# A first TensorE job in four chunks, and a new list schedule, in a hybrid decoder block

## The chip, the cores and the metric

The kernel runs on one core of a Trainium2 chip. The metric is the device time of one execution in microseconds (us). TensorE (PE in the profile, PEld its weight loads) multiplies matrices, VectorE (DVE) and ScalarE (ACT) work element by element, SyncE (SP) and GpSimd (POOL) mostly issue transfers (DMA) between memory and the on-chip buffers. TensorE writes its results into eight banks, which VectorE and ScalarE read.

## The reference

One decoder layer over 512 tokens of width 1024, with 256 memory tokens; every input is fp32.

```python
h = _rmsnorm(x, norm_mix_g)
p_a, p_b, q, p_g = jnp.split(h @ w_in, IN_SPLITS, axis=-1)
gb, gc, v = jnp.split(p_a, 3, axis=-1)
y_a = (gb * _causal_dwconv(gc * v, conv_a_w)) @ w_a_out
u, ug = jnp.split(p_b, 2, axis=-1)
u = _causal_dwconv(u * jax.nn.sigmoid(ug), conv_b_w) + conv_b_bias      # 31 taps
y_b = jax.nn.silu(_layernorm(u, ln_b_g, ln_b_b)) @ w_b_out
k, vm = jnp.split(_rmsnorm(mem, norm_mem_g) @ w_kv, 2, axis=-1)
y_c = attention(q, k, vm) @ w_att_out                                   # 4 heads
g = jax.nn.sigmoid(p_g + b_gate)
x = x + (g[0] * y_a + g[1] * y_b + g[2] * y_c) @ w_o
gt, up = jnp.split(_causal_dwconv(_rmsnorm(x, norm_ffn_g) @ w_up, conv_ffn_w), 2, axis=-1)
x = x + (jax.nn.silu(gt) * up) @ w_down
return _rmsnorm(x, norm_final_g)
```

The block touched first is `_rmsnorm(mem, norm_mem_g) @ w_kv`: the keys and values of the memory tokens.

## The kernel before, in words

**Split operands.** Each fp32 operand is split into a high part (a cast to fp32r) and a low part (the operand minus the high part). ScalarE makes the high part (whi of weights, mh of the memory block), VectorE the low part (wlo, ml). A product is then three matmuls: high by high, high by low, low by high. For weights a "unit" is a tile of 128x1024 loaded into one of six load buffers (wf); whi and wlo have four buffers each. The helper split_job makes the two jobs ("wh", unit) and ("wl", unit), at lines 495 and 499.

**Seven products for eight.** The large projections (w_in and w_up in quads of four blocks, w_o, w_down) use seven block products, numbered 1 to 7, in place of eight, on sums and differences of operands and weights. The sums of weights are mostly made by transfers that add (jobs s5, s6, s7, s3 on POOL, line 633). The jobs r1 to r7 (lines 702 to 723) read the banks into results. A job of TensorE in a quad is 24 matmuls (line 675).

**The planner.** All work is put into a table of jobs with engine, cost, what it follows and which buffers it takes. TensorE's jobs have a fixed order, and from it each other job gets a due time, the latest start that keeps TensorE going. Then a list scheduler places jobs one at a time: the one that can start earliest, and among equals the one with the earliest due time. This gives each engine's program order, which the chip then follows with waits on semaphores. Two tables change the result, both by kind of job, a key such as "SP ld up u". LATER adds so many us to a due time and so moves the job back (or, if negative, forward) in the ranking. A kind in AHEAD may not start earlier than so many us before its due time. A kind that is in neither starts as soon as it can. "NONE" jobs take no engine; "temps" closes the buffers of the mixer and opens those of the up projection.

**The start.** jobs.first is a hand-written list of the first loads; their due times are their place in it less its length, to which LATER is added. TensorE begins with a warm-up of nine matmuls (18 records, line 1766), then the first key job K(0,0), the first value job V(0,0), V(0,1), K(1,0), K(0,1) and so on. K(0,0) multiplies the first half of the transposed memory (mem block 0, four pieces of 128x256: index i or k) by the first unit of w_kv. Both arrive as two loads of 256 KB each. For the memory block the jobs ("mh", g, e) and ("ml", g, e) treat two pieces at a time (lines 765 and 772). halved_unit (line 859) does the same for K(0,0) and V(0,0): loads, casts (line 873) and low parts (line 877) in halves of 128x512. pe_keys (line 964) cuts K(0,0) into two TensorE jobs of 12 matmuls, each behind its own half.

```python
job(("mh", g, e), "ACT", 2 * scaled_act(256), mem_high,
    [("ldm", g, e)] + ([("mh", g, 0)] if e else []), use=[("mem", g)])
...
for e in range(2):
    pe(K0 if e else ("K0",), 12 * MM_QUAD,
       lambda e=e: keys_product(0, 0, (2 * e, 2 * e + 1)), [("wl0", "K", e), ("ml", 0, e)],
       take=[] if e else [(bank, "ps")], use=[bank] if e else [], unit=e == 1)
```

keys_product (line 929 holds its matmul) runs over the two halves of the result and, in each, over the pieces it was given.

## Time and profile before

| | |
|---|---|
| median of 3 runs | 925.8 us (925.8 to 926.52) |
| profiled execution, its own time | 925.64 us |
| its span, first to last instruction | 923.8 us |
| mean granted TensorE clock | 0.999 |
| instructions | 16764 |
| first product of K(0,0), last matmul | 5.30 us, 917.86 us |

Times in the profile count from the span's start. "L929" is line 929 of the kernel. A row of the timeline has start, length, engine, line, operation, what is written from what, the shapes, and how many instructions were merged; in brackets stands how long the engine idled before and what ended it. Tile names are the program's: mem and mh/ml belong to the memory block, wf to a loaded weight unit, whi/wlo to its parts, fb00 to ft7 to the seven forms of the activations (an h or l behind for the part), bank to an accumulator. SPq rows are transfers being issued.

### The profile page before, as it was taken

The page shows a single profiled execution, that of the slowest core. Times are in us where ns is not written, and L with a number is a line of the kernel's source. Part 1 is how long each engine was busy: PE and PEld are TensorE (multiplying, and loading weights), DVE is VectorE, ACT ScalarE, POOL GpSimd, SP SyncE. Part 2 cuts the span into 40 slices and gives each one's busy share as a digit, 9 for nine tenths or more (in the row PEclk, how much of TensorE's full clock was granted, in tenths as well). Part 3 has the DMA queues.
Part 4 walks back from the last instruction along what each step waited for, and adds up shares of the span by engine and source line. Part 5 has one row for each costly group of instructions (what it writes and reads, how often), then busy time and mean ns, then how long its engine had stood idle before and what let it go on. Part 6 is the DMA issues. An engine that isn't in the chain of part 4 may idle for free.

```text
span 923.8 us, 16764 instructions
## 1 busy us (share of the span) xinstructions
PE 916.6 (99%) x6677; PEld 862.8 (93%) x6677; DVE 837.4 (91%) x953; ACT 671.0 (73%) x911; POOL 126.5 (14%) x153
## 2 busy tenths in 40 slices
PE   9999999999999999999999999999999999999997
PEld 8999999999989999999899888899999999988886
DVE  6897999989989999999986779898999889999987
ACT  7567988879977887788746743777766676765656
POOL 0121121101111211110100001021221121003300
PEclk9999999999999999999999999999999999999999
DMA  9999689666787879788956598499999877789962
GB/s 364 367 252 199 151 178 205 167 160 137 194 188 205 183 168 213 174 210 201 220 108 173 157 322 187 114 227 307 279 248 226 207 142 149 197 266 338 244 131 92
DMA packets 54366, 190.60 MB, mean 206 GB/s; under 512 B 6160, under 2 KB 6544, under 8 KB 54288
## 3 DMA queue, kind: packets, MB, share of 16 engines
q0 software_dynamic: 20880, 75.24, 45.2%
q1 hardware_dynamic: 33120, 114.02, 34.7%
q8 instruction: 52, 0.85, 0.3%
q10 hardware_dynamic: 288, 0.27, 0.1%
q14 instruction: 26, 0.21, 0.1%
HBM read 185.31 MB, written 4.19 MB: 205 GB/s over the span
## 4 chain that ended last, share of the span: by engine, by line
PE 95%; DMA 2%; DVE 1%; issue 0%; ACT 0%; POOL 0%; DVEq 0%; POOLq 0%; ACTq 0%
PE bank L675 57%; PE bank L448 7%; PE bank L446 7%; PE bank L447 7%; PE bank L1418 5%; PE bank L1417 5%; PE bank L1419 5%; PE bank L929 2%; DMA wf<-in_w_up 2%; PE bank L1766 0%; PE ss L802 0%; DVE wlo L499 0%; PE bank L1166 0%; DVE upc L1373 0%; DVE gtc L1373 0%
## 5 line engine op out<-in xcount | busy, mean ns | idle before, releaser
L495 ACT CAST whi<-wf 128x1024 fp32r<-128x1024 f32 (+1 forms) x199 | 206.9, 1044 | 97.7 <-PE bank L675 39.3
L499 DVE TENSOR_TENSOR wlo<-wf,whi 128x1024 fp32r<-128x1024 f32 (+1 forms) x193 | 232.4, 1211 | 29.8 <-ACT whi L495 29.6
L1238 ACT ACTIVATE tp<-u,pk 128x510 f32<-128x510 f32 (+22 forms) x184 | 119.4, 704 | 7.0 <-DVE acc L1245 6.9
L1245 DVE TENSOR_TENSOR acc<-acc,tp 128x1020 f32<-128x1020 f32 (+22 forms) x92 | 109.2, 1188 | 6.0 <-ACT tp L1238 5.0
L633 POOL DMA_DIRECT2D wf<-in_w_in x51 | 45.1, 890 | 245.1 <-DVE wlo L499 160.2
L675 PE MATMUL bank<-ft6h,wlo 128*128 128x256 f32 x232 | 64.3, 277 | 0.1
L675 PE MATMUL bank<-fb10h,whi 128*128 128x256 f32 x232 | 64.4, 278 | 0.0
L675 PE MATMUL bank<-fb00h,whi 128*128 128x256 f32 x232 | 64.4, 278 | 0.0
L675 PE MATMUL bank<-ft6h,whi 128*128 128x256 f32 x232 | 64.4, 277 | 0.0
L675 PE MATMUL bank<-ft7h,whi 128*128 128x256 f32 x232 | 64.3, 277 | 0.0
L675 PE MATMUL bank<-ft7l,whi 128*128 128x256 f32 x232 | 64.3, 277 | 0.0
L675 PE MATMUL bank<-ft7h,wlo 128*128 128x256 f32 x232 | 64.3, 277 | 0.0
L675 PE MATMUL bank<-fb00l,whi 128*128 128x256 f32 x232 | 64.3, 277 | 0.0
L675 PE MATMUL bank<-fb11h,whi 128*128 128x256 f32 x232 | 64.3, 277 | 0.0
L675 PE MATMUL bank<-fb00h,wlo 128*128 128x256 f32 x232 | 64.3, 277 | 0.0
L675 PE MATMUL bank<-ft5h,wlo 128*128 128x256 f32 x232 | 64.3, 277 | 0.0
L675 PE MATMUL bank<-ft5h,whi 128*128 128x256 f32 x232 | 64.3, 277 | 0.0
L675 PE MATMUL bank<-ft5l,whi 128*128 128x256 f32 x232 | 64.3, 277 | 0.0
L675 PE MATMUL bank<-ft6l,whi 128*128 128x256 f32 x232 | 64.2, 277 | 0.0
L675 PE MATMUL bank<-fb10h,wlo 128*128 128x256 f32 x232 | 64.2, 277 | 0.0
L675 PE MATMUL bank<-fb10l,whi 128*128 128x256 f32 x232 | 64.2, 277 | 0.0
L675 PE MATMUL bank<-fb11l,whi 128*128 128x256 f32 x232 | 64.1, 276 | 0.0
(388 smaller groups left out, 3146.1 us busy)
## 6 DMA issues: line engine op xcount, KB each, us to landing
wf<-in_w_in SPq DMA_DIRECT2D x55, 512.0 KB, 5.1
wf<-in_w_in POOLq DMA_DIRECT2D x51, 512.0 KB, 6.2
wf<-in_w_up SPq DMA_DIRECT2D x29, 512.0 KB, 5.7
wf<-in_w_up POOLq DMA_DIRECT2D x28, 512.0 KB, 6.1
wf<-in_w_down SPq DMA_DIRECT2D x15, 512.0 KB, 3.7
wf<-in_w_att_out SPq DMA_DIRECT2D x8, 512.0 KB, 4.5
wf<-in_w_a_out SPq DMA_DIRECT2D x8, 512.0 KB, 4.2
wf<-in_w_b_out SPq DMA_DIRECT2D x8, 512.0 KB, 4.3
```

The costliest lines, as they stand in the source:

```text
L446: nc.tensor.matmul(ps, s_hi, w_hi, start=start, stop=False, skip_group_check=again)
L447: nc.tensor.matmul(ps, s_hi, w_lo, start=False, stop=False, skip_group_check=again)
L448: nc.tensor.matmul(ps, s_lo, w_hi, start=False, stop=stop, skip_group_check=again)
L495: nc.scalar.copy(parts[0], src())
L499: nc.vector.tensor_tensor(lo, src(), hi.bitcast(F32), op=ALU.subtract)
L633: nc.gpsimd.dma_start(out=tiles[key], in_=block(w, col[c], k), accum_op=ALU.add)
L675: nc.tensor.matmul(ps[:, c, :], w[:, k, at], a[k], start=first and n == 0, stop=i == 3 and n == 2, skip_group_check=again,)
L1238: nc.scalar.activation(two(("tp", p, s))[:, j, s:], two(("u", p))[:, j, : SEQ - s], AF.Copy, scale=weight(j),)
L1245: nc.vector.tensor_tensor(a, a, two(("tp", p, s))[:, :, s:], op=ALU.add)
L1417: nc.tensor.matmul(ps, w_hi[:, i, at], hi, start=first, stop=False)
L1418: nc.tensor.matmul(ps, w_hi[:, i, at], lo, start=False, stop=False)
L1419: nc.tensor.matmul(ps, w_lo[:, i, at], hi, start=False, stop=last)
```

## The change

Four edits of the code, and new tables:

1. For both memory blocks the jobs mh and ml are defined for each of the four pieces, not for two at a time. The instructions are the same, eight a side; other work can be placed between them.
2. halved_unit takes a number of pieces: the casts and low parts of K(0,0) are in quarters of 128x256 (four and four instructions for two and two), those of V(0,0) stay halves. The loads stay halves.
3. K(0,0) is four TensorE jobs of six matmuls, one for each piece k, each behind its own ("wl0", "K", k) and ("ml", 0, k). The 24 matmuls are the same; their order is now by piece, then by half of the result.
4. Later jobs on the memory blocks wait for the last piece, ("ml", g, 3), or for the second piece of their pair.
5. The tables LATER and AHEAD are replaced. LATER had 33 entries and has 39, AHEAD had 8 and has 15.

```diff
--- before.py
+++ after.py
@@ -70,19 +70,21 @@
 
 
 LATER = {
-    "ACT r1 cv": -198, "ACT r1 gate": -73, "ACT r5 gate": -106, "ACT tap 1": -3.62,
-    "ACT tp 3": -101, "ACT vh": 37, "ACT wh merge 2": -5, "ACT wh mix 5": 117,
-    "DVE fl h2 t4": 1.22, "DVE fl h2 t7": -5, "DVE h t5": 56, "DVE h2 t4": -19, "DVE kl": -60,
-    "DVE low": -20, "DVE r2 up": 19, "DVE tap 2": -32, "DVE tap 3": 136, "DVE wl up 6": -90,
-    "DVE wl up 7": -30, "DVE x1 c": -46, "DVE xnorm": 97, "SP ld K 0": -4, "SP ld V 0": -6,
-    "SP ld mix r": 13, "SP ld mix u": 12, "SP ld mix v": 10.92, "SP ld up r": -18,
-    "SP ld up s": -23.22, "SP ld up u": -64, "SP ld up v": -34, "SP ld0 K": -102,
-    "SP ld0 V": -5.56, "SP ldm": -4,
+    "ACT fh h2 t7": 5, "ACT r4 glu": -10, "ACT r5 glu": 284, "ACT sigmoid": 19.8,
+    "ACT tp 3": -37.08, "ACT wh mix 2": 109, "ACT wh up 5": 96, "DVE CV": -29, "DVE h t7": 109,
+    "DVE kl": 27, "DVE kt": 65, "DVE ql": -145, "DVE r3 cv": -1, "DVE r3 glu": 38,
+    "DVE r3 q": -26, "DVE r7 gate": -15, "DVE tap 2": -44, "DVE vl": 189, "DVE wl V 0": -4,
+    "DVE wl mix 1": -22, "DVE wl mix 2": -11, "DVE wl mix 5": 30, "DVE wl up 6": -24,
+    "DVE xnorm": 85, "NONE temps": 25, "POOL s5 glu": 30, "POOL s5 up": 6.66, "SP ld K 0": 3,
+    "SP ld e 0": -7, "SP ld mix r": 11, "SP ld mix s": -6, "SP ld mix v": 6, "SP ld up r": -42,
+    "SP ld up s": -43, "SP ld up u": -64, "SP ld up v": -44, "SP ld wo 0": -41, "SP x1b": 58,
+    "SP xl": 8,
 }
 
 AHEAD = {
-    "ACT r1 glu": 5, "ACT tap 1": 150, "ACT vh": 5, "DVE kl": 10, "DVE low": 10, "DVE tot1": 40,
-    "POOL wadd e": 5, "POOL xa": 10,
+    "ACT fh h2 t7": 10, "ACT mgh g": 5, "ACT r5 cv": 40, "ACT sigmoid": 40, "ACT tp 3": 40,
+    "DVE CV": 80, "DVE r3 cv": 5, "DVE r3 glu": 40, "NONE temps": 20, "POOL s3 q": 5,
+    "POOL s5 glu": 40, "POOL s5 up": 20, "SP ld e 0": 10, "SP x1b": 80, "SP xl": 20,
 }
 
 
@@ -756,29 +758,29 @@
                 out=tiles["mem", g][:, 512 * e : 512 * (e + 1)], in_=mem_t[2 * g + e]),
                 [("mem tile", g)], LOAD_LATENCY, use=[("mem", g)])
 
-            def mem_high(g=g, e=e):
-                if e == 0:
-                    for part, side in (("mh", "h"), ("ml", "l")):
-                        tiles[part, g] = forms.tile(
-                            [P, 4, HALF], F32R, tag=MEM_PLACE[g] + side, name=name(part))
-                for i in range(2 * e, 2 * e + 2):
+
+            for i in range(2 * e, 2 * e + 2):
+                def mem_high(g=g, i=i):
+                    if i == 0:
+                        for part, side in (("mh", "h"), ("ml", "l")):
+                            tiles[part, g] = forms.tile(
+                                [P, 4, HALF], F32R, tag=MEM_PLACE[g] + side, name=name(part))
                     nc.scalar.activation(
                         tiles["mh", g][:, i, :], four(("mem", g))[:, i, :], AF.Copy,
                         scale=par("norm_mem_g", 4 * g + i),
                     )
 
-            def mem_low(g=g, e=e):
-                for i in range(2 * e, 2 * e + 2):
+                def mem_low(g=g, i=i):
                     nc.vector.scalar_tensor_tensor(
                         tiles["ml", g][:, i, :], four(("mem", g))[:, i, :],
                         par("norm_mem_g", 4 * g + i), tiles["mh", g][:, i, :].bitcast(F32),
                         op0=ALU.mult, op1=ALU.subtract,
                     )
 
-            job(("mh", g, e), "ACT", 2 * scaled_act(256), mem_high,
-                [("ldm", g, e)] + ([("mh", g, 0)] if e else []), use=[("mem", g)])
-            job(("ml", g, e), "DVE", 2 * 0.4, mem_low,
-                [("mh", g, e)] + ([("ml", g, 0)] if e else []), use=[("mem", g)])
+                job(("mh", g, i), "ACT", scaled_act(256), mem_high,
+                    [("ldm", g, e)] + ([("mh", g, i - 1)] if i else []), use=[("mem", g)])
+                job(("ml", g, i), "DVE", 0.4, mem_low,
+                    [("mh", g, i)] + ([("ml", g, i - 1)] if i else []), use=[("mem", g)])
 
         def mem_square(g=g):
             make(("msq", g))
@@ -856,7 +858,7 @@
 
     K0, V0 = ("K", 0, 0), ("V", 0, 0)
 
-    def halved_unit(unit, src, n_k):
+    def halved_unit(unit, src, n_k, pieces):
         s, raw, parts = unit[0], ("raw", unit), []
         job(("raw tile", s), "NONE", 0.0, lambda: make(raw), take=[(raw, "wf")])
         for e in range(2):
@@ -865,25 +867,27 @@
                 out=tiles[raw][:, at], in_=src[:, at]), [("raw tile", s)],
                 LOAD_LATENCY, use=[raw])
 
-            def high(e=e, at=at):
-                if e == 0:
+        width = 1024 // pieces
+        for i in range(pieces):
+            def high(i=i, at=slice(width * i, width * (i + 1))):
+                if i == 0:
                     parts.extend(
                         wts.tile([P, 1024], F32R, tag=s, name=name(s)) for s in ("whi", "wlo"))
                     w_units[unit] = [t.rearrange("p (k n) -> p k n", k=n_k) for t in parts]
                 nc.scalar.copy(parts[0][:, at], tiles[raw][:, at])
 
-            def low(at=at):
+            def low(at=slice(width * i, width * (i + 1))):
                 hi, lo = parts
                 nc.vector.tensor_tensor(
                     lo[:, at], tiles[raw][:, at], hi[:, at].bitcast(F32), op=ALU.subtract
                 )
 
-            job(("wh0", s, e), "ACT", actv(512), high,
-                [("ld0", s, e)] + ([("wh0", s, 0)] if e else []), use=[raw])
-            job(("wl0", s, e), "DVE", dve(512), low, [("wh0", s, e)], use=[raw])
-
-    halved_unit(K0, block(w_kv, 0, 0), 4)
-    halved_unit(V0, w_v[0, 0], 2)
+            job(("wh0", s, i), "ACT", actv(width), high,
+                [("ld0", s, 2 * i // pieces)] + ([("wh0", s, i - 1)] if i else []), use=[raw])
+            job(("wl0", s, i), "DVE", dve(width), low, [("wh0", s, i)], use=[raw])
+
+    halved_unit(K0, block(w_kv, 0, 0), 4, 4)
+    halved_unit(V0, w_v[0, 0], 2, 2)
 
     for hp in range(2):
         for kp in range(4):
@@ -946,7 +950,7 @@
 
     def pe_values(hp, kp):
         banks = [("bank", "V", hp, c) for c in range(MC)]
-        take, lows = [(b, "ps") for b in banks], [("ml", kp // 2, kp % 2)]
+        take, lows = [(b, "ps") for b in banks], [("ml", kp // 2, 2 * (kp % 2) + 1)]
         if (hp, kp) == (0, 0):
             for e in range(2):
                 pe(V0 if e else ("V0",), 6 * MM, lambda e=e: values_product(0, 0, e),
@@ -964,13 +968,13 @@
     def pe_keys(h, g):
         bank = ("bank", "K", h)
         if (h, g) == (0, 0):
-            for e in range(2):
-                pe(K0 if e else ("K0",), 12 * MM_QUAD,
-                   lambda e=e: keys_product(0, 0, (2 * e, 2 * e + 1)), [("wl0", "K", e), ("ml", 0, e)],
-                   take=[] if e else [(bank, "ps")], use=[bank] if e else [], unit=e == 1)
+            for k in range(4):
+                pe(K0 if k == 3 else ("K0", k), 6 * MM_QUAD,
+                   lambda k=k: keys_product(0, 0, (k,)), [("wl0", "K", k), ("ml", 0, k)],
+                   take=[] if k else [(bank, "ps")], use=[bank] if k else [], unit=k == 3)
         else:
             pe(("K", h, g), 24 * MM_QUAD, lambda: keys_product(h, g, range(4)),
-               [("wl", ("K", h, g)), ("ml", g, 1)], take=[] if g else [(bank, "ps")],
+               [("wl", ("K", h, g)), ("ml", g, 3)], take=[] if g else [(bank, "ps")],
                use=[bank] if g else [])
```

## The prediction

> **What bounds the kernel now.** I read the busy line of the page first, then the waits of TensorE, then the busy time by stretch.
>
> ```profile
> PE 916.6 (99%) x6677; PEld 862.8 (93%) x6677; DVE 837.4 (91%) x953; ACT 671.0 (73%) x911; POOL 126.5 (14%) x153
> ...
> PE bank L1766 <- POOL ident masks.py:199: 1.4, 1, 1.4
> ...
> 0.00:5.30 5.30, 3.94 (x19) 3.92 (x19) 0.91 (x3) 3.00 (x5) 0.77 (x8) 1.00 0.67 201
> 5.30:9.13 3.83, 3.83 (x26) 3.60 (x25) 3.48 (x6) 2.88 (x6) 0.00 (x0) 1.00 1.03 398
> ...
> 598.00:643.00 45.00, 45.00 (x383) 44.67 (x381) 39.57 (x45) 33.51 (x47) 8.61 (x10) 1.00 0.99 265
> ...
> 918.00:923.80 5.80, 0.13 (x2) 0.00 (x0) 2.13 (x5) 1.52 (x4) 0.00 (x0) 0.84 0.72 271
> ```
>
> In the stretches the columns are length, then busy time and count for PE, PEld, DVE, ACT and POOL, then clock, DMA share and GB/s. TensorE is the bound almost without a hole. Its only listed wait is before the warm-up, and from 598 to 643 us, where the transfers are densest, it is busy the whole time. A busy PE can still hide a pause of a few tenths, because the ends of matmuls are modelled, so from here on I compare starts. The number of matmuls is the same after the change, so there are three places to win: the start (first product at 5.30), pauses between neighbouring starts, and the end after the last matmul (918 to 923.8), which the edit of the code doesn't touch.
>
> The start, with all engines in order of time (start, length, engine; SPq rows are loads being issued):
>
> ```profile
> 0.74 0.39 SPq L755 DMA_DIRECT2D mem<-in_mem_t  x1
> 1.19 0.89 SPq L864 DMA_DIRECT2D wf<-in_w_kv  x2
> 1.36 4.21 PE L1766 MATMUL bank<-ident 128*128 128x128 f32 x18 [1.36 <-POOL ident masks.py:199]
> 2.12 0.43 SPq L755 DMA_DIRECT2D mem<-in_mem_t  x1
> 3.83 0.91 ACT L765 ACTIVATE mh<-mem,pk 128x256 fp32r<-128x256 f32 x2 [1.50 <-DMA pk<-in_packed]
> 4.64 0.60 ACT L873 CAST whi<-wf 128x512 fp32r<-128x512 f32 x1
> 5.28 0.69 DVE L877 TENSOR_TENSOR wlo<-wf,whi 128x512 fp32r<-128x512 f32 x1
> 5.30 0.58 PE L929 MATMUL bank<-mh,whi 128*128 128x256 f32 x1
> 5.59 0.62 ACT L873 CAST whi<-wf 128x512 fp32r<-128x512 f32 x1 [0.34 <-DMA wf<-in_w_kv]
> 5.68 0.41 PE L929 MATMUL bank<-ml,whi 128*128 128x256 f32 x1
> 6.02 0.58 PE L929 MATMUL bank<-mh,wlo 128*128 128x256 f32 x1
> 6.40 0.41 PE L929 MATMUL bank<-mh,whi 128*128 128x256 f32 x1
> 6.62 0.41 PE L929 MATMUL bank<-ml,whi 128*128 128x256 f32 x1
> 7.04 0.33 PE L929 MATMUL bank<-mh,whi 128*128 128x256 f32 x1
> 7.21 0.28 PE L929 MATMUL bank<-ml,whi 128*128 128x256 f32 x1
> 7.32 0.28 PE L929 MATMUL bank<-mh,wlo 128*128 128x256 f32 x1
> 9.13 0.39 PE L446 MATMUL bank<-whi,mh 128*128 128x512 f32 x1
> ```
>
> The first product starts just after the first half of whi is done (4.64 + 0.60 = 5.24). The third needs wlo, done at 5.28 + 0.69 = 5.97, and starts at 6.02. Starts are 0.22 apart until about 7.04 and 0.11 apart from 7.21 on. The 24 products of the first job end where V0 begins, at 9.13.
>
> **The chunks.** With four pieces the first job waits for a quarter of each operand. Two rows price a 128x256 piece:
>
> ```profile
> 621.05 0.41 ACT L596 CAST ft4x<-h2b 128x256 fp32r<-128x256 f32 x1
> 625.08 0.42 DVE L601 TENSOR_TENSOR ft4x<-h2b,ft4x 128x256 fp32r<-128x256 f32 x1
> ```
>
> So a quarter of the weight unit costs 0.41 us on ScalarE and 0.42 on VectorE, where a half costs 0.60 to 0.62 and 0.69. Over the unit that is 4 x 0.41 - 2 x 0.61 = 0.42 us more ScalarE and 4 x 0.42 - 2 x 0.69 = 0.30 us more VectorE. The memory block keeps its eight instructions a side; only their order is free now. The first chain becomes: mh piece from 3.83, whi piece about 4.25 to 4.65 (its load had landed by 4.64), wlo piece about 4.8 to 5.2. All of it is done before 5.30. The warm-up's 18 records, some 0.22 us apart from 1.36, occupy TensorE until about 5.2 to 5.3, so the first product stays at 5.2 to 5.3; I take 5.30. The second stays at 5.68, since a weight load is exposed there (5.30 to 5.68 is 0.38, against 0.22 in the row after). The third no longer waits for wlo: 5.68 + 0.22 = 5.90 for 6.02, and the fourth, which before paid the same exposed load after the wait (6.02 to 6.40), comes at 6.12, 0.28 us earlier.
>
> What becomes of the 0.28 depends on the slow stretch. If it ends at 7.04 whatever TensorE has done, products 4 to 8 still come 0.22 apart, the eighth at 7.00 where it was at 7.21, and from there the lead is about 0.2. If it ends after a number of products, the lead stays 0.28, and 0.38 with a first product at 5.2. The lower end is nothing, if a later quarter waits; I take 0.25, between the first two.
>
> By the Trainium skill, "TensorE: Matmul & The Clock Gate", section "What's actually happening", the slow clock lasts for a budget of time and not for a number of matmuls, so removed idle time in it buys only half of itself. By that rule the sum would have the 0.2, by the count the 0.28. The trace shows one end of the slow spacing, at about 7.1, and can't tell the two apart.
>
> The later quarters mustn't wait. The list of first loads ranks the second part of the memory block ahead of the second half of K0 now that the shift of -102 on "SP ld0 K" is gone (in the rows above both K0 halves left at 1.19 and the block's second part at 2.12). The half that arrived at 5.59 then arrives one 256 KB slot later, 0.26 MB / 398 GB/s = 0.66 us: about 6.25. Then whi pieces 3 and 4 end by about 7.2 and the last wlo piece by 7.7 on VectorE; quarter 3 of TensorE starts near 7.6 and wants its wlo near 7.85, quarter 4's is wanted near 8.5. No wait, with about 0.4 us to spare; the bound of a loss here is the 0.66 slot itself.
>
> **The loads behind it.** The shifts on "SP ldm" and "SP ld K 0" change too: -4 for both before; none and +3 now. So the second memory block (two loads) goes ahead of the weights K(1,0).
>
> ```profile
> 4.02 0.43 SPq L525 DMA_DIRECT2D wf<-in_w_kv  x1
> 4.50 1.11 SPq L755 DMA_DIRECT2D mem<-in_mem_t  x2
> ...
> 10.88 1.03 ACT L495 CAST whi<-wf 128x1024 fp32r<-128x1024 f32 x1
> 11.82 0.90 ACT L765 ACTIVATE mh<-mem,pk 128x256 fp32r<-128x256 f32 x2
> 11.95 1.23 DVE L499 TENSOR_TENSOR wlo<-wf,whi 128x1024 fp32r<-128x1024 f32 x1 [0.67 <-ACT whi L495]
> ...
> 14.86 0.28 PE L929 MATMUL bank<-mh,wlo 128*128 128x256 f32 x1
> ```
>
> K(1,0) was cast at 10.88, so it had landed; behind 0.52 MB more it lands at most 0.52 / 398 = 1.3 us later, 12.2. Its wlo was done at 13.18 and would be by 14.5; it is wanted at 14.86 - 0.25 = 14.61. That is cover of 0.1 us, and mh pieces of 0.41 that slip in front eat it. The cost lies between 0 and some 1.0 us (two such pieces on each engine); I take 0, since the transfers lost to K(1,0) bring the memory block's own work forward into the idle time of ScalarE.
>
> **The new list schedule.** It touches the priorities of some sixty kinds of jobs, moves no matmul and issues no instruction more; what it can cost is a wait of TensorE. The place with least to spare is the start of the up projection, where the transfers have a DMA share of 0.99 (first fence):
>
> ```profile
> 609.67 0.59 ACT L702 COPY gt<-bank 128x512 f32<-128x512 f32 x1
> ...
> 610.57 8.41 DMA wf<-in_w_up
> ...
> 642.12 1.23 DVE wlo L499
> ...
> 601.62 0.28 PE L675 MATMUL bank<-fb10h,whi 128*128 128x256 f32 x1
> 620.34 0.28 PE L675 MATMUL bank<-ft6h,whi 128*128 128x256 f32 x1
> 642.99 0.28 PE L675 MATMUL bank<-ft6l,whi 128*128 128x256 f32 x1
> 643.39 0.38 PE L675 MATMUL bank<-ft6h,wlo 128*128 128x256 f32 x1
> ```
>
> At 643.39 TensorE starts 0.40 after its neighbour instead of 0.11: 0.29 us lost to a wlo that ended at 643.35. So the split of (up 2, product 6) has no cover at all, and the edit changes its shift ("DVE wl up 6" from -90 to -24), those of the four kinds of up loads, and holds back "temps", after which the first banks of the up projection are read. That hold can be worked out from the code: the read at 609.67 must let the bank of (up 0, product 2), which starts at 601.62 and lasts 2.8, be read within 8 us of its end; that makes its due time about 601.6 + 2.8 + 8 - 1.4 = 611 (1.4 is what the code's costs give the read and the add behind it), and +25 - 20 moves it to 616. The bank is written again at 620.34, so about 4 us are left: no cost by itself. What is queued behind it on ScalarE and VectorE moves later with it, towards 642. For the whole schedule the bounds are a gain of 0.29 (that pause gone) and a loss of one landing, 8.4 us. I take 0 for the forecast.
>
> **The sum.** Profiled execution: 925.64 us (span 923.8 and 1.84 around it). First job -0.25, loads behind it 0, schedule 0: 925.4. The runs shown have a median of 925.8, 0.16 above the profiled one; carried over, 925.8 - 0.25 = 925.5. Own range of this case: 925.8 - 0.38 - 0.29 = 925.1 to 925.8.
>
> **The rivals.**
>
> No gain: K(1,0) or the last quarter of K0 comes late and eats the lead, 0.25 to 1.0 us. For it: a cover of 0.1 and 0.4 us. Against it: idle time of ScalarE near there (0.34 before 5.59). Time 925.8 to 926.6.
>
> A transfer takes the place of the wait, at the start of the up projection. A load of w_up queued one place later lands with the next one; TensorE, which has no spare time at 643, stands still for a landing less what neighbouring units have spare. Price from 2.8 us (one job of 24 products, the time by which units are staggered) to 8.4 (the chain's row): 928.6 to 934.2, middle 931. It decides from the point where the wlo of product 6 is over 2 us later than 643.35. For it: the DMA share of 0.99 and four changed loading shifts. Against it: the loads and the split keep negative shifts, so they still go before most else.
>
> Held reads: one of the kinds now held back (r3 and r5, s5, sigmoid, temps) frees its bank or its unit late, and TensorE waits one job's 2.8 us for it, once or twice: 928.6 to 931. For it: fifteen kinds of job now have such a hold, eight had one before. Against it: at the one hold worked out 4 us are left.
>
> Clearly faster: it would need 1.9 us, but start (0.38) and pause (0.29) give 0.67. Only a gain after 918, with 5.8 us of which the edit moves none, could add to it.
>
> **Chances.** Forecast 0.40; no gain 0.13; transfer 0.28; held reads 0.15; clearly faster 0.04. A measurement of this kernel can tell about 0.2% (1.9 us) from no change, so the first two are "same", 0.53; the next two slower, 0.43; faster 0.04. The likeliest case's own range is 925.1 to 925.8. With two signs in play the range for 8 in 10 runs from 924.8 to 933: it leaves out the dearer part of the transfer case and the clearly faster one.
>
> **What would show it.** Right: third product about 0.22 after the second, V0's first matmul near 8.9 for 9.13, K(1,0) following V(0,1) without a pause, starts in 598 to 660 us spaced as before, and the last matmul some 0.25 us earlier. The clock's part: whether the spacing still changes near 7.04. The no-gain case: a gap before wlo products near 8 or 14.6. The transfer case: TensorE's idle time between 600 and 680 with a w_up transfer or a wlo ahead of it in the chain of waits. Held reads: a pause of TensorE that ends with a ScalarE copy or a VectorE add out of a bank. The prediction is wrong if TensorE pauses for over 2 us in sum anywhere after 20 us, or the tail after its last matmul grows.

## The result, and the profile after

The changed kernel takes 927.53 us (median of 15 runs, 926.37 to 929.06), the kernel before 925.8 us (15 runs, 925.17 to 926.58). The ratio is 1.0019 with a 95% interval of 1.0011 to 1.0027: the change costs about 1.7 us. The profiled execution took 928.13 us, 2.49 more than that of the kernel before.

First the busy line of the page after, the waits of TensorE (engine, line, what was waited for: us in total, times, longest), and two stretches with the columns of the prediction's first fence:

```profile
PE 917.6 (99%) x6677; PEld 863.0 (93%) x6677; DVE 838.9 (91%) x955; ACT 670.3 (72%) x913; POOL 126.9 (14%) x153
...
PE bank L1770 <- POOL ident masks.py:199: 1.4, 1, 1.4
PE bank L933 <- DVE wlo L501: 0.8, 1, 0.8
PE bank L677 <- ACT gt L704: 0.4, 1, 0.4
PE bank L449 <- DVE wlo L501: 0.2, 1, 0.2
...
9.13:20.00 10.87, 9.84 (x60) 8.35 (x60) 8.76 (x11) 10.50 (x14) 0.00 (x0) 1.00 1.03 421
598.00:643.00 45.00, 45.00 (x377) 44.52 (x376) 40.48 (x46) 33.32 (x48) 8.68 (x10) 1.00 0.99 253
```

The busy time grew by only 1.0 us (916.6 before). The waits list three new entries, two of them before 20 us. From 9.13 to 20 us TensorE started 60 matmuls, where the kernel before started 74:

```profile
9.13:20.00 10.87, 10.87 (x74) 9.88 (x73) 9.28 (x11) 10.72 (x14) 0.00 (x0) 1.00 1.03 416
```

To see where each tenth goes I take, for the same matmul in both timelines, its start in one kernel minus its start in the kernel before. I call this the lag; the columns are times of the kernel before, in us. (In the order of its matmuls K(0,0) differs with the change; from V0 on the matmuls correspond one to one.)

| execution | V0 9.13 | 14.63 | 14.86 | 20.0 | 44.5 | 66 | 104 | 140 | 158 | 640 | 917.8 |
|---|---|---|---|---|---|---|---|---|---|---|---|
| changed kernel, profiled | -0.71 | -0.10 | +0.85 | +1.14 | +1.34 | +1.97 | +2.31 | +2.31 | +2.32 | +2.28 | +2.25 |

So the head came 0.7 us early, most of the lead was gone by 14.6, one step of 0.95 came at 14.86, smaller growth up to 80 us, and nothing that lasts after that. The growth of 0.97 between 44.5 and 104 us is not waiting: no start there is late against its neighbour, and TensorE ran two stretches at a slower pace (last section). The up projection, where the prediction looked for its largest danger, adds nothing in the end.

The head, in order of time (start, length, engine):

```profile
1.36 3.79 PE L1770 MATMUL bank<-ident 128*128 128x128 f32 x18 [1.36 <-POOL ident masks.py:199]
4.69 0.70 ACT L877 CAST whi<-wf 128x256 fp32r<-128x256 f32 x2
5.13 0.39 PE L933 MATMUL bank<-mh,whi 128*128 128x256 f32 x1
...
5.36 0.28 PE L933 MATMUL bank<-ml,whi 128*128 128x256 f32 x1
5.69 0.38 PE L933 MATMUL bank<-mh,wlo 128*128 128x256 f32 x1
5.91 0.28 PE L933 MATMUL bank<-mh,whi 128*128 128x256 f32 x1
6.04 0.28 PE L933 MATMUL bank<-ml,whi 128*128 128x256 f32 x1
6.11 0.41 ACT L877 CAST whi<-wf 128x256 fp32r<-128x256 f32 x1 [0.32 <-DMA wf<-in_w_kv]
8.42 0.40 PE L448 MATMUL bank<-whi,mh 128*128 128x512 f32 x1
```

The quarters do what they say. The third product starts at 5.69, 0.33 us behind the second, since the first wlo quarter is only just done, and 0.33 us earlier than before. The second half of K0 is cast from 6.11, after a short wait for its load, and no later quarter holds TensorE for more than a tenth (8.06 is 0.20 behind its neighbour). The spacing drops to 0.12 from 5.91 on, in the kernel before only from 7.21. But the chunks are not the only difference: the 18 records of the warm-up took 3.79 us here and 4.21 before, since TensorE's fast clock had begun during the warm-up in this execution (last section).

Behind it, the path to K(1,0): its loads being issued (SPq rows), then ScalarE, VectorE and TensorE:

```profile
4.02 1.02 SPq L757 DMA_DIRECT2D mem<-in_mem_t  x2
5.08 1.41 SPq L527 DMA_DIRECT2D wf<-in_w_kv  x2
...
10.46 0.51 ACT L768 ACTIVATE mh<-mem,pk 128x256 fp32r<-128x256 f32 x1
10.87 1.04 ACT L787 ACTIVATE msq<-mem 128x1024 f32<-128x1024 f32 x1
...
11.82 0.49 ACT L768 ACTIVATE mh<-mem,pk 128x256 fp32r<-128x256 f32 x1
12.22 1.05 ACT L787 ACTIVATE msq<-mem 128x1024 f32<-128x1024 f32 x1
13.17 1.99 ACT L497 CAST whi<-wf 128x1024 fp32r<-128x1024 f32 x2
...
14.44 2.35 DVE L501 TENSOR_TENSOR wlo<-wf,whi 128x1024 fp32r<-128x1024 f32 x2
14.64 0.28 PE L933 MATMUL bank<-ml,whi 128*128 128x256 f32 x1
15.71 0.39 PE L933 MATMUL bank<-mh,wlo 128*128 128x256 f32 x1 [0.79 <-DVE wlo L501]
```

The second memory block now goes ahead of K(1,0), in its loads (4.02 and 5.08) and on both engines. The cast of K(1,0) starts at 13.17, where it started at 10.88; its low part starts at 14.44 for 11.95 and, as the first of two, ends near 15.6; and the third matmul of K(1,0) starts at 15.71, 1.07 after its neighbour instead of 0.11. The load is only a part of this. Issued at 5.08, it landed 6.9 us later, near 12.0, where it had landed near 10.2 before; the cast began 1.2 us after the landing, behind the square of 12.22 on ScalarE.

### The profile page after: what moved, and what is told of

Same layout as the page of the kernel before. It is cut to its first block, busy times and chain, and to the rows that moved or that the text cites. A ratio compares the mean times of both kernels' runs of the same rounds, so it can differ in the third digit from the quotient of the medians.

```text
span 926.1 us, 16782 instructions
## 1 busy us (share of the span) xinstructions
PE 917.6 (99%) x6677; PEld 863.0 (93%) x6677; DVE 838.9 (91%) x955; ACT 670.3 (72%) x913; POOL 126.9 (14%) x153
## 4 chain that ended last, share of the span: by engine, by line
PE 94%; DMA 3%; issue 1%; ACT 1%; DVE 0%; SPq 0%; DVEq 0%; POOLq 0%
PE bank L677 57%; PE bank L448 7%; PE bank L450 7%; PE bank L449 7%; PE bank L1421 5%; PE bank L1422 5%; PE bank L1423 5%; DMA wf<-in_w_up 2%; PE bank L933 2%; DMA wf<-in_w_v 1%; PE ss L804 0%; PE bank L1170 0%; ACT whi L497 0%; PE bank L1659 0%; DVE wlo L501 0%
## 5 line engine op out<-in xcount | busy, mean ns | idle before, releaser
L497 ACT CAST whi<-wf 128x1024 fp32r<-128x1024 f32 (+1 forms) x195 | 202.6, 1046 | 89.0 <-PE bank L677 31.5
L501 DVE TENSOR_TENSOR wlo<-wf,whi 128x1024 fp32r<-128x1024 f32 (+1 forms) x189 | 227.9, 1212 | 23.5 <-ACT whi L497 23.2
L1242 ACT ACTIVATE tp<-u,pk 128x511 f32<-128x511 f32 (+22 forms) x184 | 119.7, 710 | 11.7 <-DVE acc L1249 11.3
L1249 DVE TENSOR_TENSOR acc<-acc,tp 128x1002 f32<-128x1002 f32 (+22 forms) x92 | 109.0, 1189 | 7.1 <-ACT tp L1242 5.1
L635 POOL DMA_DIRECT2D wf<-in_w_in x48 | 42.3, 888 | 227.4 <-DVE wlo L501 139.4
```

What stands on the lines that cost most here:

```text
L497: nc.scalar.copy(parts[0], src())
L501: nc.vector.tensor_tensor(lo, src(), hi.bitcast(F32), op=ALU.subtract)
L635: nc.gpsimd.dma_start(out=tiles[key], in_=block(w, col[c], k), accum_op=ALU.add)
L1242: nc.scalar.activation(two(("tp", p, s))[:, j, s:], two(("u", p))[:, j, : SEQ - s], AF.Copy, scale=weight(j),)
L1249: nc.vector.tensor_tensor(a, a, two(("tp", p, s))[:, :, s:], op=ALU.add)
```

## The experiments

The new order has several places with no cover. The first question was which half of the change costs: the chunks or the tables. So each was made alone, and then the thin places were mended one by one.

**The old tables on the new code.**

```diff
-LATER = {  "ACT fh h2 t7": 5, ... }      # 39 entries of the changed kernel
+LATER = {  "ACT r1 cv": -198, ... }      # 33 entries of the kernel before
-AHEAD = {  "ACT fh h2 t7": 10, ... }
+AHEAD = {  "ACT r1 glu": 5, ... }
```

> The code of the change (chunks, TensorE's first job in four) with LATER and AHEAD of the kernel before. Theory (the chunks give a lead of 0.2 to 0.8 us and all loss is in the new tables): 925.0 to 925.6 us, ratio 0.9992 to 0.9998. Rival (the code itself loses, by more instructions and a different order that the planner makes of finer jobs): 926.5 or more, ratio over 1.0008.

Measured: 930.62 us (929.44 to 931.59, 5 runs), ratio 1.0054 [1.0042, 1.0066], slower than the changed kernel. The first row of its waits of TensorE shows the larger part:

```profile
PE bank L1657 <- DVE xnorm L1649: 2.7, 1, 2.7
```

The wait for xnorm lies near 596 us, the lag goes up by 2.9 there; before, that place had no wait. Another 1.2 us is lost at 18.5, where K(0,1) waits for an ml piece that stands behind a wlo on VectorE. The only difference from the kernel before is in the jobs of the first 20 us, and with it the planner's list comes out otherwise 580 us later. A set of tables belongs to one table of jobs, so this run does not say what the chunks cost.

**The new tables on the old code**, the same exchange the other way round.

> The code of the kernel before with the LATER and AHEAD of the change. Theory (the loss is in the tables): slower than the changed kernel by the lead that the chunks give, 928 to 929 us, ratio 1.002 to 1.003. Rival (the tables need the finer jobs to lose or to win): 925.5 to 926.5, ratio within 1.0008 of 1.

Measured: 927.13 us (926.81 to 929.03, 11 runs), ratio 1.0020 [1.0011, 1.0028]. Without any chunk the loss is that of the whole change. In its trace the lag is +0.50 at 14.86, +1.42 at 66 and +1.64 at the end.

**The chunks in the old order.** The jobs, their costs and the tables are those of the kernel before; only inside the jobs of K(0,0) the casts and low parts are in quarters and the products run by piece.

```diff
-                nc.scalar.copy(parts[0][:, at], tiles[raw][:, at])
+                for p in pieces(at):
+                    nc.scalar.copy(parts[0][:, p], tiles[raw][:, p])
...
-                   lambda e=e: keys_product(0, 0, (2 * e, 2 * e + 1)), [("wl0", "K", e), ("ml", 0, e)],
+                   lambda e=e: [keys_product(0, 0, (k,)) for k in (2 * e, 2 * e + 1)], [("wl0", "K", e), ("ml", 0, e)],
```

> The kernel before with its own tables and its own finished order; only the first job is cut: the casts and low parts of K(0,0) in quarters inside the jobs that made halves, and the products of K(0,0) by piece. Every other instruction stands where it stood. Theory (the chunks alone give a lead, the new order loses it): first product near 5.1 and V(0,0) near 8.5 to 8.8; the lead of 0.3 to 0.7 us lasts to the end, 925.0 to 925.4 us, ratio 0.9992 to 0.9997. Rival (the lead is eaten by the next thing that transfers time, at 9 to 20 us or at the wait near 643 us): lag 0 against the kernel before from there on, ratio 0.9998 to 1.0003.

Measured: 925.27 us (924.38 to 925.81, 11 runs) against 925.5, ratio 0.9996 [0.9987, 1.0006]. The lag is -0.35 at V0, +0.03 at 14.86 and 20, and -0.25 at the end, nearly all of it gained near 643. With the chunks and no new order the loss is gone; a gain can't be told from none. So the loss belongs to the new order.

**K(1,0) first.** To change one place of an order and no other, the planner's finished list is kept and replayed, and a job is taken out of it and put ahead of another. With an empty list of moves every engine has the order of the kernel it was made from.

```diff
+MOVES = [(("ld", ("raw", ("K", 1, 0))), ("ldm", 1, 0)), (("wh", ("K", 1, 0)), ("mh", 1, 0)),
+         (("wl", ("K", 1, 0)), ("ml", 1, 0))]
...
+    def emit(self, planned):
+        for key, ahead_of in MOVES:
+            at = next(i for i, p in enumerate(planned) if p[0] == key)
+            job = planned.pop(at)
+            to = next(i for i, p in enumerate(planned) if p[0] == ahead_of)
+            planned.insert(to, job)
```

> The changed kernel with three jobs moved in the finished order and nothing planned anew: the load of K(1,0) ahead of the second memory block's loads, its cast ahead of the first mh of that block, its low part ahead of the block's first ml, as the kernel before has them. Theory (the order of the start takes the time): the wait of 0.96 us before the third matmul of K(1,0) at 14.6 is gone, the lag against the kernel before falls by about 1.0 us from there to the end: 927.5 - 1.0 = 926.5 us, ratio to before about 1.0008. Rival (the lead comes back elsewhere: what follows waits for something timed by transfers, not by TensorE): TensorE stands still by as much before 45 us and the time stays 927.3 to 927.7, ratio 1.0019.

Measured: 927.12 us (926.18 to 928.48, 11 runs), ratio 1.0016 [1.0008, 1.0025]. The wait at K(1,0) is gone (lag -0.33 at 14.63 and -0.32 at 14.86), and the next one shows, at K(0,1). VectorE and TensorE, from the timeline of this run:

```profile
17.00 1.22 DVE L520 TENSOR_TENSOR wlo<-wf,whi 128x1024 fp32r<-128x1024 f32 x1
18.14 0.48 DVE L793 SCALAR_TENSOR_TENSOR ml<-mem,pk,mh 128x256 fp32r<-128x256 f32 x1
...
18.07 0.28 PE L952 MATMUL bank<-mh,whi 128*128 128x256 f32 x1
18.67 0.38 PE L952 MATMUL bank<-ml,whi 128*128 128x256 f32 x1 [0.33 <-DVE ml L793]
```

An ml piece now stands behind the wlo of 17.00 and is done at 18.62; TensorE wanted it at 18.18. The lag at 20 is +0.27 for +1.14. From 44 to 66 us it then grows to +1.07. The median is 1.6 us above its own runs of the kernel before (925.55), where that of the change is 1.7 above: no gain that the intervals can tell. K(0,1) is also where the old tables on the new code lost their 1.2 us, so the finer pieces have a thin cover there under either set of tables.

**fb00l first.** The second thin place is the first GLU product at 43.5. In the kernel before, the low part fb00l is made early, in the new order last, behind the weights' low parts. VectorE and TensorE in the changed kernel:

```profile
42.04 1.66 DVE L1005 SCALAR_TENSOR_TENSOR hb<-x,pk,rows 128x256 f32<-128x256 f32 x4
43.61 1.22 DVE L603 TENSOR_TENSOR fb00l<-hb,fb00h 128x1024 fp32r<-128x1024 f32 x1
...
44.69 0.28 PE L677 MATMUL bank<-fb00h,whi 128*128 128x256 f32 x1
44.89 0.39 PE L677 MATMUL bank<-fb00l,whi 128*128 128x256 f32 x1
```

and VectorE in the kernel before:

```profile
40.20 1.22 DVE L601 TENSOR_TENSOR fb00l<-hb,fb00h 128x1024 fp32r<-128x1024 f32 x1
```

fb00l ends at 44.83 and is used at 44.89; before, it was done by 41.42 and used at 43.66. A cover of 2.2 us became a start 0.09 later than the usual 0.11 after its neighbour. The edit puts fb00l ahead by moving the weights' part behind it:

```diff
+MOVES = [(("wl", (("glu", 0), 2)), ("wl", ("K", 3, 0)))]
```

> The changed kernel with one VectorE job moved in the finished order: the low part of the unit (glu 0, product 2) goes behind fb00l instead of ahead of the last part of the normalisation, so fb00l is done about 1.1 us earlier, near 43.7. Theory (a wait of 0.1 us at 44.9 puts TensorE into a slower pace, 118 ns a matmul for 113, until about 77): no wait there, 113 ns from 45 us on, 1.1 to 1.3 us less in all: about 926.3 us, ratio 1.0006. Rival (the pace comes from the traffic of the other engines and the transfers at that time, not from the wait): the pace stays at 118 until about 77 and only the 0.1 us of the wait goes: 927.4 us, ratio 1.0018.

Measured: 927.43 us (926.05 to 931.34, 12 runs), ratio 1.0024 [1.0014, 1.0033]: no gain in the median. In the profiled execution, of 926.23 us, the place has no wait and the lag stays at +0.36 from 20 to 140; the step at K(1,0) is there (+0.60).

**The opposite: the kernel before with fb00l made late**, its other work unchanged.

```diff
+MOVES = [(("wl", (("glu", 0), 1)), ("fl", "h", "b00")), (("fl", "h", "b10"), ("fl", "h", "b00"))]
```

> The kernel before with one thing moved in the finished order: the low parts of (glu 0, product 1) and of fb10 go ahead of fb00l on VectorE, so fb00l is done near 43.9 us, some 0.2 to 0.3 us after TensorE first wants it at 43.66; nothing else changes. Theory (a short wait sets the slower pace): 118 ns a matmul from 44 us to about 75 instead of 113, the wait plus 0.8 to 1.1 us: ratio 1.0011 to 1.0015. Rival (pace from traffic): 113 ns as before, only the wait: ratio 1.0002 to 1.0003.

Measured: 926.45 us (925.64 to 928.33, 11 runs), ratio 1.0010 [1.0001, 1.0018]. One thin place put into the old order goes with 0.95 us more in the median, by an interval that only just leaves out 1, and with wider runs. Its trace:

```profile
42.40 1.22 DVE L620 TENSOR_TENSOR fb00l<-hb,fb00h 128x1024 fp32r<-128x1024 f32 x1
...
43.23 0.28 PE L694 MATMUL bank<-fb00h,whi 128*128 128x256 f32 x1
43.67 0.38 PE L694 MATMUL bank<-fb00l,whi 128*128 128x256 f32 x1 [0.16 <-DVE fb00l L620]
```

The lag goes from -0.32 at 20 to +0.12 at 44.5 and to +0.72 at 66, more than the wait itself (the last section tells of that). It does not last in this execution: the lag is +0.70 at 600, +0.07 at 640 and +0.04 at the end, and the execution took 925.64 us, as long as the profiled one of the kernel before. So the trace shows the wait and the slower pace behind it, and not that they reach the end.

**Both places mended.**

```diff
 MOVES = [(("ld", ("raw", ("K", 1, 0))), ("ldm", 1, 0)), (("wh", ("K", 1, 0)), ("mh", 1, 0)),
-         (("wl", ("K", 1, 0)), ("ml", 1, 0))]
+         (("wl", ("K", 1, 0)), ("ml", 1, 0)), (("wl", (("glu", 0), 2)), ("wl", ("K", 3, 0)))]
```

> The changed kernel with both sets of moves, K(1,0) as in e1 and the low part of (glu 0, product 2) as in e2. Theory (the two waits add up): lag near 0 at 20 us, TensorE at 113 ns from 45 us, 2.0 us less than the changed kernel: about 925.6 us, ratio 0.9995 to 1.0003. Rival (the loss comes back later, near 150 or at 640 us, as the medians of e1 and e2 hint): 926.5 to 927.2 us, ratio 1.001 to 1.0017, with waits of TensorE after 100 us.

Measured: 926.69 us (925.66 to 929.71, 11 runs) against 925.5, ratio 1.0017 [1.0008, 1.0026]. The median is 1.2 us above its own runs of the kernel before, where the change's is 1.7 above; by the ratio (1.0017 against 1.0019) nearly nothing is back, and the intervals overlap.

**The up projection's old entries, on top of that.** The entries of LATER and AHEAD for up, h2, xnorm, temps and x1 c are those of the kernel before; the orders differ only from about 540 us on.

> The kernel of e6 (the changed kernel with its two waits of the start moved away), and in LATER and AHEAD the entries for the start of the up projection (kinds of up and h2, xnorm, temps, x1 c) as the kernel before has them; the order differs from e6 only from about 545 us on. Theory (what e6 still loses against the kernel before, about 1.2 us by the medians, comes from varying waits at the dense transfers of 600 to 660 us, which the new entries made tighter): ratio 0.9995 to 1.0003, and no single execution over 928. Rival (it is lost before 545 us): ratio 1.0010 to 1.0017 as e6.

Measured: 927.02 us (926.06 to 928.83, 11 runs) against 925.53, ratio 1.0015 [1.0006, 1.0024]: nothing gained. The theory that the rest is lost between 600 and 660 us fell. The trace shows where it went in this execution instead; ScalarE and TensorE:

```profile
106.43 0.57 ACT L724 COPY ug<-bank 128x512 f32<-128x512 f32 x1
...
106.62 0.28 PE L682 MATMUL bank<-ft5h,wlo 128*128 128x256 f32 x1
107.05 0.38 PE L682 MATMUL bank<-ft7h,whi 128*128 128x256 f32 x1 [0.15 <-ACT ug L724]
```

The changed kernel makes the same copy at the same time:

```profile
106.66 0.58 ACT L719 COPY ug<-bank 128x512 f32<-128x512 f32 x1
```

There nobody waits for it, since TensorE, 2.3 us behind, wants the bank later. This is one reason for the small gains: TensorE, set free at one place, arrives early at the next, whose time is set by ScalarE's queue or by a transfer.

**Further executions**, two of the changed kernel and one with both places mended, each with its own profile, to see how steady the places are.

> The changed kernel again, for the trace of another execution. Theory (the waits at 14.6 and 44.9 and the slow pace behind the second are in every execution; what differs between executions is the start's clock and a wait of 0 to 2 us near 600 to 660): waits of TensorE at the third matmul of K(1,0) and at fb00l, 118 ns from 45 to 77 us. Rival (they were chance in the first trace): at least one of the two is missing.

> As e9: a third execution of the changed kernel, with the same two expectations.

> The kernel of e6 again, for the trace of another execution (its times went from 925.7 to 929.7, its trace was of 926.2). Theory (a varying wait near 600 to 660 us): in a slower execution the lag against the kernel before grows there, in one as fast as the first it stays near 0.4. Rival (it grows elsewhere): a step of the lag over 0.5 us outside 600 to 660.

Measured: 926.82, 926.26 and 927.73 us. The lags of these and of two earlier executions:

| execution | V0 9.13 | 14.63 | 14.86 | 20.0 | 44.5 | 66 | 104 | 140 | 158 | 640 | 917.8 |
|---|---|---|---|---|---|---|---|---|---|---|---|
| changed, second execution | -0.03 | +0.07 | +0.37 | +0.48 | +0.65 | +0.66 | +0.66 | +0.65 | +1.02 | +0.95 | +1.12 |
| changed, third execution | -0.76 | -0.55 | +0.41 | +0.52 | +0.69 | +0.70 | +0.70 | +0.69 | +0.70 | +0.66 | +0.44 |
| both places mended | -0.10 | -0.11 | -0.10 | +0.34 | +0.33 | +0.34 | +0.34 | +0.34 | +0.59 | +0.53 | +0.38 |
| both mended, second execution | +0.23 | +0.24 | +0.25 | +0.70 | +0.70 | +0.71 | +0.71 | +0.71 | +1.34 | +1.64 | +1.84 |
| old up entries | -0.31 | -0.32 | -0.31 | +0.16 | +0.15 | +0.16 | +0.45 | +1.12 | +1.25 | +1.19 | +0.97 |

The step at K(1,0) is in every execution of the changed kernel (+0.95, +0.30, +0.96) and in none with K(1,0) mended. Where TensorE is earlier at 140 than in the first profile, a further step can come at 155. Its rows in the second execution of the changed kernel, on GpSimd, ScalarE, VectorE and TensorE:

```profile
142.91 1.76 POOL L635 DMA_DIRECT2D wf<-in_w_in  x2 [3.53 <-PE bank L677]
...
154.12 1.05 ACT L497 CAST whi<-wf 128x1024 fp32r<-128x1024 f32 x1 [2.62 <-DMA wf<-in_w_in]
155.21 1.22 DVE L501 TENSOR_TENSOR wlo<-wf,whi 128x1024 fp32r<-128x1024 f32 x1 [1.17 <-ACT whi L497]
156.14 0.28 PE L677 MATMUL bank<-fb11l,whi 128*128 128x256 f32 x1
156.49 0.39 PE L677 MATMUL bank<-fb11h,wlo 128*128 128x256 f32 x1
```

Two adding transfers are issued one right behind the other at 142.91 and landed 5.9 and 10.6 us later; the weights of (glu 3, product 3) are cast only at 154.12, after ScalarE idled 2.6 us for them, and TensorE loses 0.24. In the kernel before, the first adding transfer of this place is issued alone at 142.19, the next at 151.47, and the low part was made at 152.00. That the pair is slow because its two transfers go together was not tried. In the profiled execution of the changed kernel the cast comes at 154.28, as late as here, but TensorE is late too and doesn't wait; in the third execution, with a lag of +0.69, the slower of the two took 9.2 us and there is no step.

**The chunks in the old order, with the pause at 643 taken away.**

```diff
+MOVES = [(("wl", (("up", 2), 6)), ("z", 0))]
```

> The kernel of e5 (the order of the kernel before, first job in quarters) with one more move in the finished order: the low part of (up 2, product 6) goes ahead of the product z of up 0 on VectorE, so it is done about 1.1 us earlier, near 642.3. Theory (both gains hold to the end): the lag against the kernel before is -0.1 to -0.3 us up to 640 and 0.25 to 0.3 us more from 643.4 on; 0.4 to 0.6 us less than before in all, ratio 0.9994 to 0.9996. Rival (z comes late and its readers, or the next low part, wait): the lag returns to that of e5 by 660 us, ratio 0.9996 to 1.0001.

Measured: 925.38 us (924.62 to 925.98, 11 runs) against 925.37, ratio 1.0001 [0.9992, 1.0009]. The lag is -0.28 at V0, -0.04 at 20 and -0.29 at the end. No version here beats the kernel before by more than its interval.

**Four places at once**: the moves of both mended places, the last pieces of mem block 1 ahead of the weights of V(0,2), and the adding transfers s6 and s7 of q and s5 of the gate at another place in POOL's queue, behind that of (glu 3, product 3). In addition s6 of q is held until the weights of (glu 3, product 3) are cast.

```diff
+MOVES += [(("mh", 1, 3), ("wh", ("V", 0, 2))), (("ml", 1, 3), ("wl", ("V", 0, 2))),
+          (("s6", ("q", 0)), ("wl", (("glu", 3), 3))), (("s7", ("q", 0)), ("wl", (("glu", 3), 3))),
+          (("s5", ("gate", 2, 0)), ("wl", (("glu", 3), 3)))]
+PACED = {("s6", ("q", 0)): ("wh", (("glu", 3), 3))}
```

> The kernel of e6 with two more thin places of the first 160 us thickened: the last mh and ml of the second memory block go ahead of the split of V(0,2), and the adding transfer s6 of (q 0) is issued only when the weights of (glu 3, product 3) have landed and are cast, not beside their transfer. Theory (the loss is a handful of thin covers in the first 160 us): no step of the lag at 18.5 and 155.6 us, lag under 0.3 from 20 us to 640, ratio 0.9998 to 1.0006. Rival (with these thickened others come forward, as the covers of the new order are thin all along): the lag still grows by over 0.5 us between 20 and 640, ratio 1.0010 or more.

Measured: 932.27 us (930.21 to 933.22, 5 runs), ratio 1.0068 [1.0055, 1.0082]: a miss, by a wait of my own making. Its waits, and two stretches:

```profile
PE bank L699 <- ACT tp L1264: 3.7, 1, 3.7
...
150.00:155.00 5.00, 1.33 (x12) 1.13 (x10) 4.96 (x8) 3.15 (x5) 0.05 (x1) 0.87 0.97 175
155.00:160.00 5.00, 4.93 (x23) 4.96 (x24) 5.00 (x5) 3.38 (x6) 0.86 (x1) 0.50 0.81 238
```

With the transfers moved and held TensorE stands for 3.7 us from 151 to 155, as in no other run; which of the moves, or the hold, makes this wait was not tried. Up to there the run still answers something: the lag is -0.01 from 20 to 66, so the places of the first 66 us are mended, and then it is +0.23 at 104, +1.05 at 140 and +1.28 at 150, where the changed kernel's lag doesn't grow. In this run TensorE, on time, meets waits that it had been too late to meet.

## Why the prediction was wrong, point by point

The forecast was no measurable change, 0.3 us on the faster side; the kernel became slower by more than its interval. The time lies inside the stated range, but not for the reason that the range gave.

- **The head: right in its waits, too large in its size, and without effect on the end.** In the profiled execution the first product is at 5.13, the second at 5.36, the third at 5.69 with a wait of about a tenth for its wlo (5.90 was forecast), and a later quarter costs a tenth at most. But this execution had the fast clock from the warm-up on. The second execution of the changed kernel had it from 7.09, as the kernel before from 7.21: there the third product starts at 5.95 for 6.02, the fourth at 6.29 (6.12 was forecast for 6.40), and V0 at 9.10 for 9.13, a lead of 0.03 for the 0.25 of the sum. (The working has a slip here: half of 0.28 is 0.14, not the 0.2 that it gives to the rule.) So the 0.71 us at V0 needed the early clock. The head of the kernel before with an early clock (the run with fb00l late, from 4.90) has V0 at 8.79; the old code with the new tables and the earliest clock has it at 9.16. How chunks and clock share the lead is not separated: over the twelve executions with quarters V0 began at 8.88 on average, over the three without at 9.03, 0.15 apart, with 8.37 to 9.36 in the one and 8.79 to 9.16 in the other. And the lead is not carried on: with the chunks alone in the old order the lag at 20 us is +0.03 and -0.04. What follows V0 comes from the stretch with a DMA share of 1.03, in which the next units are not there earlier.
- **"The loads behind it", taken as 0 with bounds 0 and 1.0: this is the step that failed.** The arithmetic of the cover (0.1 us) was right; the choice of the lower bound was not. The argument was that the memory block's work would fill ScalarE's idle time. It did not. The load itself landed near 12.0, as the bound of 12.2 had it, but the cast of K(1,0) began 1.2 us later still (1.1 in the two further executions): the new order puts two mh pieces and both squares of the memory block, 0.51 + 1.04 + 0.49 + 1.05 us, on ScalarE between the cast of V(0,1)'s weights and that of K(1,0), where one square stood before. Measured: +0.30 to +0.96 at 14.86, and +0.44 to +0.59 from 14.86 to 20 in the executions where K(1,0) is mended and K(0,1) isn't.
- **"Schedule 0": failed as well, and looked in the wrong place.** Of the whole new order I examined the up projection, the place with the least cover of the old one. Covers had become thin elsewhere: fb00l from 2.2 us to none (43.5), the ug copies (68 to 106), the adding transfers (155). Each costs 0.2 to 0.6 us in the executions that wait there. In the profiled execution the slower pace adds 0.97 us to that, and no wait precedes its second stretch. From 640 to the end the lag changed by -0.4 to +0.2 us.
- **The rivals.** "No gain" had the right mechanism and place, K(1,0) late, with a price of 0.25 to 1.0; it gave 925.8 to 926.6, and the rest comes from the further places and the pace. A stall on a w_up transfer did not happen. "Held reads" appeared in small, as waits of some tenths for a ScalarE copy out of a bank (gt, ug), never as a job's 2.8 us. "Clearly faster" was rightly put out of reach.
- **The tail** did not change: the lag at the last matmul is 2.25 and the span grew by 2.3.

What is shown: the loss goes with the new tables (1.0020 with the old code) and not with the chunks (0.9996); the step at K(1,0) has its cause in the order of loads and pieces, since moving its load, cast and low part together removes it (the three were not moved one by one). A late fb00l alone goes with 1.0010 [1.0001, 1.0018], and its trace does not carry the loss to the end. What stays open: which places make up the 1.2 to 1.5 us that remain in the medians once K(1,0) and fb00l are mended. Two executions of that kernel differ in this (+0.59 and +1.34 at 158, +0.38 and +1.84 at the end), and the run that mended further places carried a new wait. How much of the medians is the slower pace, worth 0.97 us in one execution of the changed kernel and nothing at the same place in two others, stays open too.

## What to carry to other kernels

Where an engine is busy 99% of the time, ask of a new order not whether the tightest old place survives but what cover each first use of a tile has in the new one, and begin with the first tens of microseconds, where loads are the bound. Thin places lie in series and hide one another: mending one buys only the way to the next, so a gain has to be read from the lag at the end and not from the wait that went away. One trace's lag also holds chance, here 0.7 us at the head and up to 1 us of pace, so the medians decide. A table of shifts tuned for one set of jobs need not suit another: the old tables on the new code took 930.62 us, more than either kernel.

## What the runs showed of the hardware

**TensorE has two paces at full clock, and a short pause can go with the slower one.** Rows of the chain of waits (start, length, what, how many matmuls), the changed kernel and then the kernel before:

```profile
44.85 5.84 PE bank L677 x48
50.69 5.65 PE bank L933 x48
56.35 2.83 PE bank L677 x24
...
64.69 104.04 PE bank L677 x912
```

```profile
43.70 5.47 PE bank L675 x48
49.17 5.44 PE bank L929 x48
54.61 2.72 PE bank L675 x24
...
62.83 103.59 PE bank L675 x912
```

5.65 / 48 is 117.7 ns a matmul, 5.44 / 48 is 113.3. The clock is 1.00 in both. The first three rows of each differ by 0.37 + 0.21 + 0.11 = 0.69 us, which is the lag's growth from 44.5 to 66 (0.63) and a part of a wait. The slower pace followed the wait for fb00l in the changed kernel's profile, with K(1,0) mended, with the new tables on the old code, and in the kernel before with fb00l late; it did not follow the same wait in the two further executions of the changed kernel (lag +0.65 and +0.66, +0.69 and +0.70). It also comes without a wait: the 912 matmuls of the last row took 0.45 us longer in the changed kernel, most of it between 65 and 79 us, where its starts are 0.118 apart and those of the kernel before 0.113. The kernel before runs at it elsewhere (5.66 for 48 from 598.96, and 0.118 from 610 to 634 us); with fb00l late most of its starts in that last stretch were 0.113 apart, which is where that execution won its 0.6 us back. What sets the pace is open. The Trainium skill, "TensorE: Matmul & The Clock Gate", section "Wait — 56ns, not 53.3ns?", has one pace once warm, the columns over 2.4 GHz and about 2.5 ns, which by an estimate from that page would be 109.2 ns for 256 columns; both measured paces are above it, and the measurement decides.

**The fast clock begins at another time in each execution.** The spacing of the matmuls shows it: the records of the warm-up are 0.21 to 0.22 apart at first, and 0.11 apart once it is fast. In the kernel before, the warm-up is slow to its end and the spacing falls at 7.21, within K(0,0). In the changed kernel it falls at 4.65 in the profiled execution, within the warm-up, at 7.09 in the second and at 4.94 in the third. Over fifteen executions it falls between 4.43 and 7.33, the earliest with the old code and the new tables. V0 of those three comes at 8.42, 9.10 and 8.37. So some 0.7 us of a single trace's head is chance. The Trainium skill, same page, section "What's actually happening", says that the window which releases the clock runs freely, so that the transition varies by about 0.5 us either way; the trace agrees in kind, with 2.9 us between its extremes.

**A pause of 3.7 us costs more than itself.** After it the granted clock was 0.50 for the stretch from 155 to 160 (second row of the last experiment's stretches, 23 matmuls where there are 46 otherwise). The lag was +1.28 ahead of the pause, +5.2 at its end, and +7.8 when the spacing was back at 0.11, near 160.6: 2.6 us on top of the pause.
